# Expert numbers by thresholds and sums over ranks, expert groups block by block in turns, and an index table of two copies

## The chip, the cores and the metric

The kernel runs on one core of one Trainium2 chip. A core has five engines that run side by side, each with a queue of its own that is worked off in order: TensorE (PE, matmuls, with PEld for its weight loads), VectorE (DVE), ScalarE (ACT), GpSimd (POOL) and SyncE (SP, which only issues DMAs here). The metric is the device time of one execution in microseconds (us); lower is better. The kernel before takes 1928.7 us, the median of three runs (1924.66 to 1932.57).

## The reference

The program is two small transformer blocks over 256 tokens of width 1024 (float32): a mixer, a cross-attention and a PEER feed-forward layer in the first, two layers with a delta-rule mixer, an attention and a feed-forward net in the second. The change lies in the PEER layer. Each token has 8 retrieval heads; each head picks 16 out of 16384 experts by product keys.

```python
def peer_ffn(h, wq, subkeys, u, v):
    q = (xt @ wq).reshape(T, PEER_HEADS, 2, PEER_HALF)
    s = jnp.einsum('thpc,hpnc->thpn', q, subkeys).astype(jnp.float32)   # 2 x 128 scores a head
    s_top, i_top = lax.top_k(s, PEER_TOPK)                              # the 16 best of each half
    cand = s_top[:, :, 0, :, None] + s_top[:, :, 1, None, :]            # 16 x 16 sums
    cand_idx = i_top[:, :, 0, :, None] * PEER_N_KEYS + i_top[:, :, 1, None, :]
    best, pos = lax.top_k(cand.reshape(T, PEER_HEADS, PEER_TOPK * PEER_TOPK), PEER_TOPK)
    experts = jnp.take_along_axis(cand_idx.reshape(...), pos, axis=-1)
    gates = jax.nn.softmax(best, axis=-1).astype(h.dtype)
    # for every chosen expert e: y += gate * gelu(u[e] . x) * v[e]
```

## The kernel before

Activations lie with features on the 128 partitions and tokens along the row. Nearly all of the time goes to products with float32 weights at two-part precision: a class `Stream` brings all weights in one stream, 8 blocks of 128x128 to a tile, and splits each tile into a rounded part `whi` (ACT, L229) and the rest `wlo` (L231, a subtraction on DVE or POOL by the pattern `W.pat`; "DDP" means two tiles on DVE and the third on POOL). `mm3` (L253 to L256) makes three matmuls of each block: whi with the high part of the activations, whi with their low part, wlo with the high part. A tile feeds 24 matmuls. `whi` and `wlo` have three buffers each (`WB`), so ACT can write the `whi` of tile n+3 only when PE is done with tile n.

The PEER layer computes all 16384 experts for all tokens and masks them: `uphase` makes gelu(u.x) for 128 groups of 128 experts, two groups into the halves of one PSUM bank (`ps`), and `vphase` sums the products with v into four banks (`ys`). Phases run in the order u 0-64, u 64-96, v 0-32, u 96-128, v 32-64, v 64-128 (`PHASES`).

While PE does u 0-64, `topk` finds the experts on DVE, 128 tokens at a time (`tt` is 0 or 1). `both(uphase(0, 64), chain(topk...), TKR)` interleaves them when the program is written: after every tile of `uphase` (a `yield`), `TKR` (1.65) steps of `topk`, each ending in a `yield` of its own. `pace` lets a step's first instruction stand only behind the last DVE split of a tile. A framework then fixes the order on each engine. One call of `topk` does this:

- `top16` for 16 half-heads: the 16 best of 128 scores and their places (`top`, `idx`), by MAX8, FIND_INDEX8 and MATCH_REPLACE8.
- The 50 sums that can be among the 16 best of 256 (`PAIRS`: rank a of the first half goes with ranks 0 to 16/(a+1)-1 of the second) into `cv` on DVE, and their expert numbers into `ce` on POOL (L840).
- `top16` again for 8 heads over the 50 sums; `pos` is the place of each of the 16 winners in the 50, `psf` its float16 copy (L849).
- The expert number of each winner: for each head a table `eq` of 50 x 16 comparisons of `psf` with a counter `iom` (DVE, L856), its product with `ce` (`hit`, POOL, L860), and a sum over the 50 (`ex`, DVE, L864). Then the number is split into its first and second key, `f1` and `f2` (L871 to L875).
- The softmax of the gates.

Later `gates` builds the mask of the chosen experts from transposed `f1` and `f2`, on DVE and PE, beside u 64-96 and v 32-64.

Of the kernel before, what the change touches and what calls it, by code (L numbers as in the profile page):

```python
# [34 lines left out]
KC = 8  # L35
T1 = 256
# [8 lines left out]
LAG, MIXR, TKR, DLR = 2, 1.15, 1.65, 4  # L45
EXPAT = "DDP"
# [20 lines left out]
def _consts():  # L67
    i = np.arange(128)
    f = np.float32
    out, at = {}, {}  # L70
# [3 lines left out]
    c1, out = out, {}  # L74
# [24 lines left out]
    for s in (1, 2, 4, 8, 16, 32, 64):  # L99
        j, q = i[:, None], i[None, :]  # L100
# [3 lines left out]
    k = np.arange(T2)  # L104
# [36 lines left out]
def tile_two_blocks(ctx, tc, ws, xT, memT, metaT, par_d, wsm_d, subk_d, c1_d, cm_d, c2_d, out, dumps=None):  # L141
    nc = tc.nc
    dumps = dumps or {}
    V, G, A, PE = nc.vector, nc.gpsimd, nc.scalar, nc.tensor
# [99 lines left out]
    W = Stream()  # L244
# [497 lines left out]
    with tc.tile_pool(name="pe", bufs=1) as mp:  # L742
# [4 lines left out]
        nh, nl = operands(T1)  # L747
# [5 lines left out]
        iota = C1("iota")  # L753
# [48 lines left out]
        with tc.tile_pool(name="tk", bufs=1) as tp:  # L802
            def pace(r):

                after(r, W.last)
# [9 lines left out]
            NCAND = 50  # L815
            iom = tp.tile([128, NCAND, 8], F16, name="iom")
            V.tensor_copy(iom, iota[:, :NCAND].unsqueeze(2).to_broadcast([128, NCAND, 8]))

            fin = {}

            def topk(tt):
                top = tp.tile([128, 16, 16], F32, name="top")
                idx = tp.tile([128, 16, 16], U32, name="idx")
# [6 lines left out]
                iv = idf.rearrange("p (h z) k -> p h z k", z=2)  # L830
                V.tensor_scalar(iv[:, :, 0], iv[:, :, 0], 128.0, None, op0=OP.mult)
                cv = tp.tile([128, 8, NCAND], F32, name="cv")
                ce = tp.tile([128, 8, NCAND], F32, name="ce")
                o = 0
                for a, na, nb in PAIRS:
                    for e, dst, src in ((V, cv, tv), (G, ce, iv)):
                        d = dst[:, :, o:o + na * nb].rearrange("p h (a b) -> p h a b", a=na)
                        x = src[:, :, 0, a:a + na].unsqueeze(3).to_broadcast([128, 8, na, nb])
                        y = src[:, :, 1, :nb].unsqueeze(2).to_broadcast([128, 8, na, nb])
                        e.tensor_add(d, x, y)  # L840
                    o += na * nb
                    yield
# [7 lines left out]
                ex = tp.tile([128, 8, 16], F32, name="ex")  # L850
                W.pat = EXPAT
                hits = {}
                for h in range(9):
                    if h < 8:
                        eq = tp.tile([128, NCAND, 2, 8], F16, name="eq", bufs=2)
                        pace(V.tensor_tensor(eq, psf[:, h].rearrange("p (a b) -> p a b", a=2).unsqueeze(1).to_broadcast(  # L856
                            [128, NCAND, 2, 8]), iom.unsqueeze(2).to_broadcast([128, NCAND, 2, 8]),
                            op=OP.is_equal))
                        hits[h] = tp.tile([128, 16, NCAND], F32, name="hit", bufs=2)
                        G.tensor_mul(hits[h], eq.rearrange("p c a b -> p (a b) c"),  # L860
                                     ce[:, h].unsqueeze(1).to_broadcast([128, 16, NCAND]))
# [9 lines left out]
                V.tensor_copy(eu, ex.rearrange("p h k -> p (h k)"))  # L871
                V.tensor_scalar(i1, eu, 7, None, op0=OP.logical_shift_right)
                V.tensor_copy(f1, i1)
                V.tensor_scalar(i1, eu, 127, None, op0=OP.bitwise_and)
                V.tensor_copy(f2, i1)  # L875
# [713 lines left out]
def layout(a):  # L1589
# [7 lines left out]
    uT = a["peer_u"][0].reshape(128, 128, 8, 128).transpose(1, 2, 3, 0).reshape(128, 8, 128, 128)  # L1597
# [66 lines left out]
```

## Time and profile before

| what | value |
|---|---|
| median of three runs | 1928.7 us (1924.66 to 1932.57) |
| the profiled execution | 1923.93 us, its span 1922.2 us |
| PE busy | 1833.0 us, 95% of the span |
| DVE, ACT, POOL busy | 1327.3, 865.3, 645.8 us |
| granted TensorE clock, mean | 0.975 of full speed |
| the chain that ended last | PE 73%, DVE 20%, issue 4%, ACT and POOL 1% each |

Busy time of PE counts matmuls that overlap, so two stretches are better compared by how many matmuls they hold. A window's count takes in matmuls that cross its edges, some two per window. All times below are from this one execution; its stages are found by the tile names: u 0-64 runs from 351.6 to 553.5 us, u 96-128 from 766 to 857 us, the last v phase from 984 us on.

### The profile page before, as it was taken

To read this page: it belongs to the slowest core of one execution; us is meant where nothing else is said; L and a number is where in the kernel's file an instruction comes from. 1 tells how busy PE (TensorE), PEld (TensorE's weight loads), DVE (VectorE), ACT (ScalarE), POOL (GpSimd) and SP (SyncE) were. 2 spreads that over 40 slices of the span, in tenths; PEclk is the share of its full clock that TensorE was granted. 3 is DMA by queue.
4 is the path that set the end of the run, shared out by engine and by line. 5 is a ranking of instruction groups with operands and counts; after the bars stand their busy time and mean duration, and the time that the engine had idled before them with its cause. 6 is when DMAs were issued, how large, how long until landed. Compare 5 with 4: busy or idle time off the path is not lost.

```text
span 1922.2 us, 36981 instructions
## 1 busy us (share of the span) xinstructions
PE 1833.0 (95%) x15387; PEld 1766.3 (92%) x15387; DVE 1327.3 (69%) x2445; ACT 865.3 (45%) x1343; POOL 645.8 (34%) x394
## 2 busy tenths in 40 slices
PE   7999999989899999998899998899999999999999
PEld 6988999989898899998899998899899998679999
DVE  7746657789899965239965557854789845658872
ACT  5456554444343344443244444332444445644442
POOL 4312322364643322223322224321244431124442
PEclk9999999999999999999999998989999999989999
DMA  6432434444443355553355553211344543124453
GB/s 226 166 120 88 145 119 176 163 167 171 159 157 132 138 188 190 184 179 130 127 175 190 193 198 124 88 54 58 130 156 176 176 176 132 45 88 174 172 183 131
DMA packets 43128, 285.58 MB, mean 149 GB/s; under 512 B 5712, under 2 KB 8528, under 8 KB 9040
## 3 DMA queue, kind: packets, MB, share of 16 engines
q1 hardware_dynamic: 42960, 283.21, 41.8%
q8 instruction: 121, 1.98, 0.4%
q14 instruction: 47, 0.39, 0.1%
HBM read 282.14 MB, written 1.05 MB: 147 GB/s over the span
## 4 chain that ended last, share of the span: by engine, by line
PE 73%; DVE 20%; issue 4%; ACT 1%; POOL 1%; DMA 0%; SPq 0%; POOLq 0%; DVEq 0%; ACTq 0%
PE ps L254 16%; PE ps L256 16%; PE ps L255 16%; DVE wlo L231 5%; PE y L255 5%; PE y L256 5%; PE y L254 5%; DVE q L926 3%; DVE as L936 2%; DVE p L921 2%; DVE cy L979 1%; PE pa L1449 1%; DVE eq L923 1%; ACT whi L229 1%; DVE cy L437 1%
## 5 line engine op out<-in xcount | busy, mean ns | idle before, releaser
L229 ACT ACTIVATE whi<-raw 128x1024 fp32r<-128x1024 f32 x527 | 557.6, 1059 | 766.7 <-PE ps L255 506.5
L231 POOL TENSOR_TENSOR wlo<-raw,whi 128x1024 fp32r<-128x1024 f32 x190 | 473.9, 2494 | 914.6 <-ACT whi L229 914.4
L256 PE MATMUL ps<-xnh,wlo 128*128 128x256 f32 (+2 forms) x2336 | 678.0, 290 | 23.5 <-POOL wlo L231 15.8
L254 PE MATMUL ps<-xnh,whi 128*128 128x256 f32 (+2 forms) x2336 | 680.7, 292 | 13.8 <-ACT whi L225 6.8
L255 PE MATMUL ps<-xnl,whi 128*128 128x256 f32 (+2 forms) x2336 | 676.3, 290 | 0.8 <-DVE xnl L334 0.8
L231 DVE TENSOR_TENSOR wlo<-raw,whi 128x1024 fp32r<-128x1024 f32 x337 | 461.4, 1369 | 265.1 <-ACT whi L229 263.2
L256 PEld LDWEIGHTS ps<-xnh,wlo 128*128 128x128 f32 x2336 | 454.1, 194 | 29.6 <-POOL wlo L231 17.4
L254 PEld LDWEIGHTS ps<-xnh,whi 128*128 128x128 f32 x2336 | 454.1, 194 | 17.2 <-ACT whi L229 7.1
L255 PEld LDWEIGHTS ps<-xnl,whi 128*128 128x128 f32 x2336 | 453.1, 194 | 3.0 <-issue 1.6
L255 PE MATMUL y<-hl,whi 128*128 128x256 f32 x1024 | 285.5, 279 | 7.7 <-DVE hl L406 7.7
L254 PE MATMUL y<-hh,whi 128*128 128x256 f32 x1024 | 287.5, 281 | 0.0
L256 PE MATMUL y<-hh,wlo 128*128 128x256 f32 x1024 | 284.7, 278 | 1.7 <-DVE wlo L231 1.7
L255 PEld LDWEIGHTS y<-hl,whi 128*128 128x128 f32 x1024 | 194.4, 190 | 9.1 <-DVE hl L406 9.1
L256 PEld LDWEIGHTS y<-hh,wlo 128*128 128x128 f32 x1024 | 194.2, 190 | 1.9 <-DVE wlo L231 1.9
L254 PEld LDWEIGHTS y<-hh,whi 128*128 128x128 f32 x1024 | 194.1, 190 | 0.0
L254 PE MATMUL ps<-fh,whi 128*128 128x272 f32 (+1 forms) x352 | 100.1, 284 | 0.0
L256 PE MATMUL ps<-fh,wlo 128*128 128x272 f32 (+1 forms) x352 | 100.1, 284 | 0.0
L255 PE MATMUL ps<-fl,whi 128*128 128x272 f32 (+1 forms) x352 | 100.0, 284 | 0.0
L406 DVE TENSOR_TENSOR hl<-as,hh 128x512 fp32r<-128x512 f32 x64 | 72.3, 1131 | 32.9 <-ACT hh L405 32.9
L979 DVE SCALAR_TENSOR_TENSOR cy<-xpad,par,cy 128x272 f32<-128x272 f32 (+1 forms) x132 | 90.2, 691 | 2.6
L254 PEld LDWEIGHTS ps<-fh,whi 128*128 128x128 f32 x352 | 66.3, 188 | 0.0
L255 PEld LDWEIGHTS ps<-fl,whi 128*128 128x128 f32 x352 | 66.3, 188 | 0.0
(527 smaller groups left out, 2728.3 us busy)
## 6 DMA issues: line engine op xcount, KB each, us to landing
raw<-in_ws_dram SPq DMA_DIRECT2D x263, 1024.0 KB, 4.8
X<-in_xT_dram SPq DMA_DIRECT2D x4, 256.0 KB, 4.5
memX<-in_memT_dram SPq DMA_DIRECT2D x1, 1024.0 KB, 13.1
as<-in_subk_d_dram SPq DMA_DIRECT2D x1, 1024.0 KB, 6.9
out_dram<-X SPq DMA_DIRECT2D x4, 256.0 KB, 2.4
c<-in_c_d_dram SPq DMA_DIRECT2D x1, 793.0 KB, 4.3
cm<-in_cm_d_dram SPq DMA_DIRECT2D x1, 776.0 KB, 10.9
raw<-in_ws_dram SPq DMA_DIRECT2D x4, 128.0 KB, 4.4
```

The source lines that it names most:

```text
L229: A.activation(hi, s, AF.Copy)
L231: r = e.tensor_sub(lo, s, hi.bitcast(F32))
L254: PE.matmul(ps, wh, xh, start=start, stop=False, **k)
L255: PE.matmul(ps, wh, xl, start=False, stop=False, **k)
L256: PE.matmul(ps, wl, xh, start=False, stop=stop, **k)
L406: V.tensor_sub(lo, x, hi.bitcast(F32))
L437: V.scalar_tensor_tensor(y, xpad[:, j:j + T1], P("conv_w", 4 * m + j), y, op0=OP.mult, op1=OP.add)
L921: V.tensor_tensor(p1, index(0, 128), pairs(i1T, 128), op=OP.is_equal)
L923: V.tensor_tensor(eq, index(R * r, R), pairs(i2T, R), op=OP.is_equal)
L926: V.tensor_mul(q[:, z], eq, pairs(gT[:, z], R))
L936: V.tensor_mul(a, a, pv[:, 32 * s:32 * s + 32])
L979: V.scalar_tensor_tensor(dst, xpad[:, j:j + T], P(wname, o + j), dst, op0=OP.mult, op1=OP.add)
```

## The change

Three edits. First, `topk` finds the two keys of each winner without the expert numbers of the candidates. The 50 places are grouped by the rank of the first half, and the groups start at thresholds 0, 16, 24, 29, 33 ... (`thr`). For each winner, `ge` holds 16 comparisons "place >= threshold"; the sum of `ge` times the steps between thresholds is the start of its group, place minus start is its rank in the second half (`rb_`), the sum of `ge` times the differences of successive first indices (`d1`) is the first key, and the sum of "rank equals `rb_`" times the second indices (`d2`) is the second. A sum over 16 is made by halving (`fold`). All of it is float16 on DVE, for all 8 heads at once (2048 elements a row). The tables `d1` and `d2` hold every index twice side by side. POOL does none of it.

Second, `uphase` takes the two groups of a bank in turns, block by block (k outside, z inside), with one start flag for the bank; the weights are laid out to match. Third, `TKR` is 1.5, and the constant tile `c1` grows by 32 columns for `thr` and `dthr`.

```diff
-LAG, MIXR, TKR, DLR = 2, 1.15, 1.65, 4
-EXPAT = "DDP"
+LAG, MIXR, TKR, DLR = 2, 1.15, 1.5, 4
...
+    thr = np.concatenate([[0], np.cumsum([16 // (a + 1) for a in range(15)])]).astype(f)
+    out["thr"] = np.broadcast_to(thr[None], (128, 16)).copy()
+    out["dthr"] = np.broadcast_to(np.diff(thr, prepend=f(0))[None], (128, 16)).copy()
...
-                for z in range(2):
-                    for k in range(KC):
+                for k in range(KC):
+                    for z in range(2):
                         wh, wl = W.block()
-                        mm3(ps[:, z * T1:(z + 1) * T1], wh, wl, nh[:, k], nl[:, k], k == 0, k == KC - 1)
-                    yield
+                        mm3(ps[:, z * T1:(z + 1) * T1], wh, wl, nh[:, k], nl[:, k], k == 0 and z == 0, k == KC - 1,
+                            skip_group_check=True)
+                    if k % 4 == 3:
+                        yield
...
-            iom = tp.tile([128, NCAND, 8], F16, name="iom")
-            V.tensor_copy(iom, iota[:, :NCAND].unsqueeze(2).to_broadcast([128, NCAND, 8]))
-
+
+            thr, dthr, rank = (tp.tile([128, 16, 16], F16, name=n) for n in ("thr", "dthr", "rank"))
...
-                idf = tp.tile([128, 16, 16], F32, name="idf")
-                V.tensor_copy(idf, idx)
+
+                iv = idx.rearrange("p (h z) k -> p h z k", z=2)
+                ix = tp.tile([128, 2, 8, 16], F16, name="ix")
+                V.tensor_copy(ix, iv.rearrange("p h z k -> p z h k"))
+                d1 = tp.tile([128, 8, 16, 2], F16, name="d1")
+                d2 = tp.tile([128, 8, 16, 2], F16, name="d2")
+                V.tensor_copy(d1[:, :, 0], ix[:, 0, :, :1].to_broadcast([128, 8, 2]))
+                for e in range(2):
+                    V.tensor_sub(d1[:, :, 1:, e], ix[:, 0, :, 1:], ix[:, 0, :, :15])
+                V.tensor_copy(d2, ix[:, 1].unsqueeze(3).to_broadcast([128, 8, 16, 2]))
+                yield
...
-                for h in range(9):
-                    if h < 8:
-                        eq = tp.tile([128, NCAND, 2, 8], F16, name="eq", bufs=2)
-                        pace(V.tensor_tensor(eq, psf[:, h].rearrange("p (a b) -> p a b", a=2).unsqueeze(1).to_broadcast(
-                            [128, NCAND, 2, 8]), iom.unsqueeze(2).to_broadcast([128, NCAND, 2, 8]),
-                            op=OP.is_equal))
-                        hits[h] = tp.tile([128, 16, NCAND], F32, name="hit", bufs=2)
-                        G.tensor_mul(hits[h], eq.rearrange("p c a b -> p (a b) c"),
-                                     ce[:, h].unsqueeze(1).to_broadcast([128, 16, NCAND]))
-                        yield
-                    if h:
-                        pace(V.reduce_sum(ex[:, h - 1], hits.pop(h - 1), axis=AX.X))
-                        yield
...
+                def fold(x, out):
+
+                    n = 8
+                    while n > 1:
+                        V.tensor_add(x[:, :, :n], x[:, :, :n], x[:, :, n:2 * n])
+                        n //= 2
+                        if n == 4:
+                            yield
+                    V.tensor_add(out, x[:, :, 0], x[:, :, 1])
+                    yield
+
+                ge, x = cells("ge"), cells("gx")
+                pace(V.tensor_tensor(ge, slots16(psf), over_h(thr), op=OP.is_ge))
+                yield
+                pace(V.tensor_mul(x, ge, over_h(dthr)))
+                yield
+                rb_ = tp.tile([128, 8, 16], F16, name="rb_")
+                yield from fold(x, rb_)
+                V.tensor_sub(rb_, psf, rb_)
+                weighted(x, ge, d1)
+                yield
+                yield from fold(x, f1.rearrange("p (h k) -> p h k", h=8))
+                pace(V.tensor_tensor(ge, slots16(rb_), over_h(rank), op=OP.is_equal))
+                yield
+                weighted(x, ge, d2)
+                yield
+                yield from fold(x, f2.rearrange("p (h k) -> p h k", h=8))
```

Two places in the order of the instructions. The first is VectorE from the eighth head's last step to the gates, for the first 128 tokens. Before:

```order
L849 CAST psf<-pos 128x128
L856 TENSOR_TENSOR eq<-psf,iom 128x800
L231 TENSOR_TENSOR wlo<-raw,whi 128x1024
L856 TENSOR_TENSOR eq<-psf,iom 128x800
L864 TENSOR_REDUCE ex<-hit 128x16
L231 TENSOR_TENSOR wlo<-raw,whi 128x1024
L856 TENSOR_TENSOR eq<-psf,iom 128x800
L864 TENSOR_REDUCE ex<-hit 128x16
L856 TENSOR_TENSOR eq<-psf,iom 128x800
L231 TENSOR_TENSOR wlo<-raw,whi 128x1024
L864 TENSOR_REDUCE ex<-hit 128x16
```

VectorE in the changed kernel (`gx` is the tile that `fold` halves, `d_4381` is `d1`; the split of a weight tile is now on L234):

```order
L858 CAST psf<-pos 128x128
L889 TENSOR_TENSOR ge<-psf,thr 128x2048
L891 TENSOR_TENSOR gx<-ge,dthr 128x2048
L881 TENSOR_TENSOR gx<-gx 128x8x128
L881 TENSOR_TENSOR gx<-gx 128x8x64
L234 TENSOR_TENSOR wlo<-raw,whi 128x1024
L881 TENSOR_TENSOR gx<-gx 128x8x32
L885 TENSOR_TENSOR rb__4813<-gx 128x128
L895 TENSOR_TENSOR rb__4813<-psf,rb__4813 128x128
L234 TENSOR_TENSOR wlo<-raw,whi 128x1024
L873 TENSOR_TENSOR gx<-ge,d_4381 128x2048
```

From the first comparison to the last sum six splits of weight tiles stood before, a seventh behind them; now four stand there, a fifth behind, and at most five `topk` instructions lie between two splits. Nothing on VectorE waits for GpSimd's `hit` any more.

The second place is GpSimd over the whole of u 0-64. Before, for the first 128 tokens:

```order
L840 TENSOR_TENSOR ce<-idf 128x8x8
L231 TENSOR_TENSOR wlo<-raw,whi 128x1024 x3
L860 TENSOR_TENSOR hit<-eq,ce 128x800 x3
L231 TENSOR_TENSOR wlo<-raw,whi 128x1024
L860 TENSOR_TENSOR hit<-eq,ce 128x800 x3
L231 TENSOR_TENSOR wlo<-raw,whi 128x1024
L860 TENSOR_TENSOR hit<-eq,ce 128x800 x2
L231 TENSOR_TENSOR wlo<-raw,whi 128x1024 x5
```

In the changed kernel GpSimd has this between the squares of the PEER norm and those of the next block's norm:

```order
L359 TENSOR_TENSOR sq<-X 128x256 x2
L234 TENSOR_TENSOR wlo<-raw,whi 128x1024
L359 TENSOR_TENSOR sq<-X 128x256
L234 TENSOR_TENSOR wlo<-raw,whi 128x1024 x101
L1062 TENSOR_TENSOR gin<-X 128x256 x2
```

All 30 instructions of `ce` and `hit` are gone from its queue; only its splits of weight tiles are left.

## Rows read from the trace of the kernel before

**Rows 1.** The page's busy time by engine: us, share of the span, instructions.
```profile
PE 1833.0 (95%) x15387; PEld 1766.3 (92%) x15387; DVE 1327.3 (69%) x2445; ACT 865.3 (45%) x1343; POOL 645.8 (34%) x394
```
**Rows 2.** Windows: us, busy (x) by engine, PE clock, DMA share, GB/s.
```profile
351.60:414.10 62.50, 62.50 (x530) 62.50 (x530) 55.62 (x221) 28.23 (x33) 28.32 (x16) 1.00 0.52 183
414.10:442.00 27.90, 20.38 (x146) 19.77 (x145) 26.23 (x19) 7.81 (x9) 23.27 (x9) 0.88 0.32 113
442.00:510.20 68.20, 68.20 (x578) 68.20 (x577) 59.50 (x232) 34.16 (x39) 29.02 (x18) 1.00 0.52 182
510.20:527.30 17.10, 11.75 (x75) 11.37 (x74) 16.15 (x11) 4.15 (x5) 14.24 (x6) 0.80 0.40 138
527.30:553.50 26.20, 26.20 (x225) 26.20 (x224) 21.18 (x39) 14.36 (x16) 14.32 (x6) 1.00 0.45 162
553.50:673.00 119.50, 110.19 (x1260) 107.02 (x1259) 118.69 (x206) 40.62 (x47) 41.67 (x16) 0.99 0.40 137
```
**Rows 3.** Who waited for whom (total, times, longest us), 404-442 and 500-530.
```profile
PE ps L256 <- POOL wlo L231: 7.3, 2, 4.7
...
PE ps L256 <- POOL wlo L231: 5.3, 1, 5.3
```
**Rows 4.** GpSimd in time order: start, us, line, what [idle before].
```profile
404.03 2.44 POOL L231 TENSOR_TENSOR wlo<-raw,whi 128x1024 fp32r<-128x1024 f32 x1 [6.11 <-ACT whi L229]
...
428.23 2.33 POOL L860 TENSOR_TENSOR hit<-eq,ce 128x800 f32<-128x800 f16 x1 [0.58 <-DVE eq L856]
430.49 3.35 POOL L231 TENSOR_TENSOR wlo<-raw,whi 128x1024 fp32r<-128x1024 f32 x1
```
**Rows 5.** VectorE in time order, the same stretch.
```profile
404.13 2.43 DVE L849 CAST psf<-pos 128x128 f16<-128x128 uint32 x1
...
408.22 2.83 DVE L856 TENSOR_TENSOR eq<-psf,iom 128x800 f16<-128x800 f16 x1
...
418.09 3.36 DVE L231 TENSOR_TENSOR wlo<-raw,whi 128x1024 fp32r<-128x1024 f32 x1
421.37 0.97 DVE L864 TENSOR_REDUCE ex<-hit 128x16 f32<-128x800 f32 x1
```
**Rows 6.** Durations by line: ns min/median/max, first and last start.
```profile
L856 DVE TENSOR_TENSOR eq<-psf,iom x16: 562/1930/2828, 406.6 to 530.5; 128x800 f16<-128x800 f16 x16
L864 DVE TENSOR_REDUCE ex<-hit x16: 971/973/987, 411.0 to 535.9; 128x16 f32<-128x800 f32 x16
L849 DVE CAST psf<-pos x2: 219/1323/2427, 404.1 to 499.7; 128x128 f16<-128x128 uint32 x2
```
**Rows 7.** POOL groups of 351.6-553.5: busy us, mean ns | idle before.
```profile
L860 POOL TENSOR_TENSOR hit<-eq,ce 128x800 f32<-128x800 f16 x16 | 45.2, 2825 | 10.5 <-DVE eq L856 9.9 <-PE ps L255 0.6
```
**Rows 8.** Durations of the weight splits in u 0-64, and ACT's from the page.
```profile
L231 DVE TENSOR_TENSOR wlo<-raw,whi x42: 1204/1222/3483, 358.0 to 549.1; 128x1024 fp32r<-128x1024 f32 x42
L231 POOL TENSOR_TENSOR wlo<-raw,whi x22: 2382/2427/4877, 351.7 to 551.9; 128x1024 fp32r<-128x1024 f32 x22
...
L229 ACT ACTIVATE whi<-raw 128x1024 fp32r<-128x1024 f32 x527 | 557.6, 1059 | 766.7 <-PE ps L255 506.5
```
**Rows 9.** Durations of nearby VectorE forms, as rows 6.
```profile
L923 DVE TENSOR_TENSOR eq<-io,i2T x64: 407/413/2512, 548.2 to 966.9; 128x512 f16<-128x512 f16 x64
L921 DVE TENSOR_TENSOR p<-io,i1T x64: 675/678/2927, 547.6 to 971.8; 128x1024 f16<-128x1024 f16 x64
L880 DVE TENSOR_TENSOR gt<-best x2: 271/272/274, 403.9 to 499.5; 128x128 f32<-128x128 f32 x2
L840 DVE TENSOR_TENSOR cv<-top x14: 176/200/2233, 381.5 to 478.4; 128x64 f32<-128x64 f32 x4, 128x128 f32<-128x128 f32 x2, 128x40 f32<-128x40 f32 x2, 128x32 f32<-128x32 f32 x2
```
**Rows 10.** Windows as rows 2: u 96-128, the last v phase, the cross-attention's output.
```profile
780.00:840.00 60.00, 60.00 (x510) 60.00 (x509) 17.17 (x14) 27.42 (x32) 17.12 (x8) 1.00 0.51 182
1000.00:1140.00 140.00, 140.00 (x1238) 140.00 (x1237) 73.36 (x60) 68.49 (x78) 40.81 (x17) 1.00 0.56 195
...
284.00:291.00 7.00, 7.00 (x61) 7.00 (x60) 5.53 (x11) 3.93 (x7) 1.15 (x2) 1.00 0.57 171
```

More of the change, by code (lines that the diff above doesn't have):

```diff
@@ L752, in tile_two_blocks @@
         V.tensor_copy(io2, C1("iota").unsqueeze(2).to_broadcast([128, 128, 2]))
-        iota = C1("iota")
         a0 = asub().rearrange("p a b -> p (a b)")
@@ L815, in tile_two_blocks @@
             NCAND = 50
-            iom = tp.tile([128, NCAND, 8], F16, name="iom")
-            V.tensor_copy(iom, iota[:, :NCAND].unsqueeze(2).to_broadcast([128, NCAND, 8]))
+            thr, dthr, rank = (tp.tile([128, 16, 16], F16, name=n) for n in ("thr", "dthr", "rank"))
+            for t, c in ((thr, C1("thr")), (dthr, C1("dthr")), (rank, C1("iota")[:, :16])):
+                V.tensor_copy(t, c.unsqueeze(2).to_broadcast([128, 16, 16]))
             fin = {}
@@ L826, in topk @@
                     yield
-                idf = tp.tile([128, 16, 16], F32, name="idf")
-                V.tensor_copy(idf, idx)
+                iv = idx.rearrange("p (h z) k -> p h z k", z=2)
[8 more added lines that the diff above has]
+                yield
                 tv = top.rearrange("p (h z) k -> p h z k", z=2)
-                iv = idf.rearrange("p (h z) k -> p h z k", z=2)
-                V.tensor_scalar(iv[:, :, 0], iv[:, :, 0], 128.0, None, op0=OP.mult)
                 cv = tp.tile([128, 8, NCAND], F32, name="cv")
-                ce = tp.tile([128, 8, NCAND], F32, name="ce")
                 o = 0
                 for a, na, nb in PAIRS:
[L836 to L840, printed above, removed]
+                    V.tensor_add(cv[:, :, o:o + na * nb].rearrange("p h (a b) -> p h a b", a=na),
+                                 tv[:, :, 0, a:a + na].unsqueeze(3).to_broadcast([128, 8, na, nb]),
+                                 tv[:, :, 1, :nb].unsqueeze(2).to_broadcast([128, 8, na, nb]))
                     o += na * nb
@@ L849, in topk @@
                 V.tensor_copy(psf, pos)
-                ex = tp.tile([128, 8, 16], F32, name="ex")
-                W.pat = EXPAT
-                hits = {}
-                for h in range(9):
-                    if h < 8:
-                        eq = tp.tile([128, NCAND, 2, 8], F16, name="eq", bufs=2)
-                        pace(V.tensor_tensor(eq, psf[:, h].rearrange("p (a b) -> p a b", a=2).unsqueeze(1).to_broadcast(
-                            [128, NCAND, 2, 8]), iom.unsqueeze(2).to_broadcast([128, NCAND, 2, 8]),
-                            op=OP.is_equal))
-                        hits[h] = tp.tile([128, 16, NCAND], F32, name="hit", bufs=2)
-                        G.tensor_mul(hits[h], eq.rearrange("p c a b -> p (a b) c"),
-                                     ce[:, h].unsqueeze(1).to_broadcast([128, 16, NCAND]))
-                        yield
-                    if h:
-                        pace(V.reduce_sum(ex[:, h - 1], hits.pop(h - 1), axis=AX.X))
-                        yield
@@ L866, in topk @@
-                W.pat = "DDP"
-                eu = tp.tile([128, 128], U32, name="eu")
-                i1 = tp.tile([128, 128], U32, name="i1")
                 f1 = tp.tile([128, 128], F32, name="f1", bufs=2)
                 f2 = tp.tile([128, 128], F32, name="f2", bufs=2)
[L871 to L874, printed above, removed]
@@ L875, in topk, with cells, over_h, slots16 @@
-                V.tensor_copy(f2, i1)
+                def cells(name):
+                    return tp.tile([128, 8, 16, 16], F16, name=name)
+                def over_h(c):
+                    return c.unsqueeze(1).to_broadcast([128, 8, 16, 16])
+                def slots16(x):
+                    return x.unsqueeze(2).to_broadcast([128, 8, 16, 16])
+                def weighted(x, mask, d):
+                    pace(V.tensor_mul(x.rearrange("p h j (s e) -> p (h j) s e", e=2),
+                                      mask.rearrange("p h j (s e) -> p (h j) s e", e=2),
+                                      d.rearrange("p h j e -> p (h j) e").unsqueeze(2).to_broadcast([128, 128, 8, 2])))
@@ L1596, in layout @@
            _blocks(a["peer_wq"][0])]
-    uT = a["peer_u"][0].reshape(128, 128, 8, 128).transpose(1, 2, 3, 0).reshape(128, 8, 128, 128)
+    uT = a["peer_u"][0].reshape(128, 64, 2, 8, 128).transpose(1, 3, 2, 4, 0).reshape(128, 8, 128, 128)
     vv = a["peer_v"][0].reshape(128, 128, 8, 128).transpose(1, 2, 0, 3).reshape(128, 8, 128, 128)
```

## The prediction

> **What bounds the kernel now.** I read the busy times first: PE is busy for 95% of the span, DVE for 69%, POOL for 34% [rows 1]. PE sets the end almost everywhere, so an edit on DVE or POOL is worth what PE waits for it, and no more. Next came the windows over u 0-64, where `topk` runs beside PE [rows 2]. Count matmuls there. In the first 62.5 us PE ran 530, less about two that cross the edges: 528, or 22 tiles, at 118.4 ns each, with the clock at full rate. The same pace holds from 442.0 to 510.2 (576 matmuls) and from 527.3 to 553.5 (222). Between lie two holes. The one of 27.9 us holds 144 matmuls, which take 144 x 118.3 ns = 17.0 us at the steady pace: 10.9 us lost. The one of 17.1 us holds 72, worth 8.5 us: 8.6 us lost. Together 19.5 us, and that includes the slower clock in them: the granted share is 0.88 and 0.80 there and 1.00 around, so some of the matmuls ran at 1.2 GHz in place of 2.4 after PE had stood still.
>
> The holes are where `eq`, `hit` and `ex` run. The waits name the cause: PE stood for POOL's `wlo`, 7.3 us in two pieces in the first hole and 5.3 us in one in the second [rows 3]. POOL's queue shows why [rows 4]: its split of 430.49 stood behind a `hit` of 2.33 us and then took 3.35 us where the median is 2.43 [rows 8]. DVE was late there too: a cast that takes 219 ns at its quickest took 2427 [rows 6], from 404.13 to 406.56, while POOL had a split from 404.03 to 406.47; an `eq` of 562 ns at its quickest took 2.83 us and a split 3.36 us in place of 1.22 [rows 5, 6, 8]. The reductions never grew (971 to 987 ns). So in this trace a DVE instruction with two inputs in SBUF, or this cast, and a POOL instruction exclude each other for a whole instruction.
>
> **What a late split costs.** With three buffers, ACT starts on the `whi` of tile n+3 when PE is done with tile n; two tiles, 5.68 us, are then left. ACT takes 1.06 us, DVE's split 1.22, POOL's 2.43 [rows 8]. The cover is 5.68 - 1.06 - 1.22 = 3.4 us for a DVE split and 2.2 us for one on POOL. A `hit` of 2.8 us ahead of POOL's split is more than 2.2; that is the hole.
>
> **Part 1, removed and added.** Gone for each half of the tokens: 8 `hit` on POOL (16 are 45.2 us [rows 7], so 22.6 a half) and seven `ce` additions; on DVE 8 `eq` at a median of 1.93 us (about 14 us) and 8 reductions at 0.97 (7.8 us), with five small casts and shifts.
> Added on DVE: five instructions over 2048 float16 elements. Their form (runs of at least two neighbours, the rest repeated) is that of `eq` and `p`: 407 ns for 512 elements, 678 for 1024 [rows 9], so 0.53 ns an element and 678 + 1024 x 0.53 = 1220 ns for 2048. Three foldings of 1024, 512, 256 and 128 elements: 0.68 + 0.41 + 0.27 + 0.27 = 1.63 us each, the last one at the 272 ns of a float32 addition of 128. With a subtraction: 5 x 1.22 + 3 x 1.63 + 0.27 = 11.3 us. The tables `ix`, `d1` and `d2` are five instructions of 120 to 256 elements, of 0.2 to 0.3 us by the same rows: 1.3 us. They stand beside the additions to `cv`, of which the longest took 2233 ns with a median of 200 [rows 9] while POOL had `ce`; those waits go, so I cost the tables at nothing (1.3 us a half if DVE had no slack).
>
> **What is late next.** POOL's queue holds only splits, so POOL's hole goes. DVE's eleven steps now lie among splits alone. From `psf` to the end of the gates (four small instructions, 0.9 us at the 0.2 to 0.3 of rows 9) DVE has 0.2 + 11.3 + 0.9 = 12.4 us of `topk` and six splits, 7.3 us; PE runs nine tiles meanwhile, 25.6 us, and POOL makes three splits, 7.3 us. Even if POOL and DVE never overlapped, the sum is 27.0 against 25.6: 1.4 us too much, once per half, against a cover of 3.4. At most five `topk` instructions (2.9 us) lie between two splits, with one POOL split 5.3 us, against 5.68 when the interval holds a POOL tile. I expect no hole, and leave 0.5 us a half for a split that comes late: 19.5 - 1.0 = 18.5 us gained. Ends: 19.5 if nothing waits; what the lock rival below leaves at the other.
> The Trainium skill ("SBUF — State Buffer", section Who interferes with whom) speaks against this edit: a DVE instruction with two SBUF inputs contends with a GpSimd instruction that reads SBUF, a reduction never does. The change swaps 7.8 us of reductions a half for additions that do. The rows agree on both kinds; by the rule alone the 1.4 us a half would count, and the gain would be 16.7 us.
>
> **TKR.** The chain had 100 steps (49 a half and two to finish), 64 tiles x 1.65 = 106; now 92, and 64 x 1.5 = 96. It ends at tile 61 either way: nothing.
>
> **Part 2, block by block in turns.** Matmuls, bytes and splits are the same; only the pace of PE can change. Three paces stand in the trace [rows 10], counts less two or three at the edges: u 96-128 has 508 in 60 us, 118.2 ns; the v phase 1236 in 140 us, 113.3 ns; the cross-attention's output product 58.5 in 7 us, 119.6 ns. All have 256 columns and a full clock. In v the moving operand stays for 24 matmuls while the output moves every three; in u and in the attention's product it is the reverse. The new u changes the output every three and the moving operand every six. Bounds for 1536 + 768 = 2304 matmuls (u 64-96 is left out: there DVE is busy 118.7 of 119.5 us [rows 2] and PE waits for it): (118.2 - 113.3) x 2304 = 11.3 us gained, (119.6 - 118.2) x 2304 = 3.2 us lost. Nearest is u itself, with the same tiles at the same distances; I take 2 us gained, since half of the changes of the moving operand go.
> The Trainium skill ("TensorE: Matmul & The Clock Gate", section Back-to-back issue gap) gives 262 cycles for 256 columns, 109 ns at 2.4 GHz as an estimate, whatever the order; all three rows lie above it and differ, so the trace doesn't bear it out. By it this part is worth 0 and the sum 2 us less.
>
> **Part 3, the larger constants.** 32 columns more lengthen one DMA of 793 KB by 16 KB off the path: nothing. They move every later tile by 128 bytes; see the last rival.
>
> **Sum.** 18.5 + 2 = 20.5 us off the profiled execution's 1923.9 (span 1922.2 and 1.7 around it): 1903.4. The median is 1928.7, 4.8 above that execution; from it the sum gives 1908.2. I name 1906, between the two.
>
> **Rivals.**
> Lock bound (chance 0.12): POOL's splits become late because every DVE instruction around them has two inputs. If each of the three POOL splits of a half waits a whole DVE instruction, 1.22, and holds back the next, the excess is 1.4 + 3 x 1.22 = 5.1 us; past the cover PE stops for 1.7 to 5, and the clock may fall again for some 3 (the first hole lost 10.9 us on 7.3 of waits). Price 5 to 8 us a half; gain 20.5 - 13 = 7: 1917 from the profiled execution. For it: rows 5 and 6 show such waits. Against: POOL's share of the stretch falls from 23.3 of 27.9 us to about a quarter.
> Pace of v (0.12): u 0-64 and 96-128 go to 113.3 ns; 11.3 in place of 2, 1894. For it: v's outputs take turns as u's will. Against: in v the moving operand rests four times as long.
> It doesn't do what it says (0.05): the 2048-element forms go at one element at a time, as float32 does: 1.22 us for 1024 [rows 8], 2.3 for 2048. 8 us more DVE a half, past the cover by 6; the holes stay, 1919 to 1924. Against: the innermost pairs are those of rows 9.
> Slower (0.04): the 128 bytes put PE's operands where products run at 119.6. v's 3072 matmuls lose 6.3 ns each, 19.4 us, u's 2304 lose 3.2, and some 7400 others of PE's 15387 instructions [rows 1] 1.4 each, 10 us: 33 - 18.5 = 14 slower, 1938. It decides from a v pace of 113.3 + 18.5/3072 us = 119.3 ns. For it: paces do differ between tiles of one shape. Against: all tiles move together, so distances stay.
> The rest (0.67) is the forecast, 1900 to 1913.
>
> **How the numbers follow.** 0.5% is 9.6 us, about what a measurement can tell from no change. Faster by more: the forecast, the v pace and half of the lock rival, 0.67 + 0.12 + 0.06 = 0.85. Within 0.5%: the other half of the lock and the rival of forms, 0.06 + 0.04 = 0.10. Slower: 0.05. The range must hold 8 in 10: it takes the forecast (0.67), most of the lock rival down to a gain of 8 and the upper part of the v pace: 1894 to 1917.
>
> **What would show it.** Right: 144 matmuls of the old first hole in about 17 us, granted clock 1.00 through u 0-64, no PE wait for POOL's split over 1 us, `ge` at about 1.22 us when it stands free. u 96-128 with 508 to 520 matmuls in 60 us; over 525 the v pace, under 504 a loss. v still at 1236 in 140 us; 1180 would be the last rival. The forecast is wrong if a hole of over 3 us stays in either half, or if `ge` takes over 2 us without a POOL split beside it.

## The result, and the profile after

The changed kernel takes 1905.63 us, the median of four runs (1899.51 to 1914.36), against 1926.78 for the kernel before beside it (four runs, 1924.66 to 1932.57): a ratio of 0.9889, 95% interval 0.9843 to 0.9935. The prediction said 1906, with 1894 to 1917 as its range. The profiled execution took 1907.24 us, its span 1905.5, so 16.7 us less span than before. The interval of the ratio allows a gain of 12.5 to 30.3 us, so stages are told apart by the profiles and not by the medians.

The page's busy times of the changed kernel answer to [rows 1]:
```profile
PE 1827.8 (96%) x15387; PEld 1762.8 (93%) x15387; DVE 1301.9 (68%) x2447; ACT 865.7 (45%) x1343; POOL 597.1 (31%) x364
```
POOL has lost its 30 instructions and 49 us, DVE 25 us, PE only 5 us of busy time. What fell is PE's standing still. The windows over u 0-64 show it; the columns are those of [rows 2], and the first two rows answer to its first two, the third to its fourth and fifth:
```profile
348.20:410.00 61.80, 61.80 (x530) 61.80 (x530) 50.19 (x225) 28.22 (x33) 19.52 (x8) 1.00 0.53 186
410.00:426.80 16.80, 16.80 (x146) 16.80 (x145) 16.52 (x17) 7.83 (x9) 5.76 (x3) 1.00 0.49 168
494.20:528.60 34.40, 34.40 (x297) 34.40 (x296) 31.12 (x43) 18.54 (x21) 11.06 (x5) 1.00 0.52 185
348.20:528.60 180.40, 180.40 (x1545) 180.40 (x1545) 152.90 (x515) 88.76 (x102) 56.04 (x22) 1.00 0.53 187
```
The stretch of the first hole now holds the same 146 matmuls in 16.8 us where it took 27.9, PE is busy throughout, and the granted clock is 1.00 in place of 0.88. The last row is the whole of u 0-64: 180.4 us with no gap in PE, where 351.6 to 553.5 was 201.9. The waits of this stretch (total, times, longest us; the first three) have no line for PE where [rows 3] had POOL's split; it is POOL and DVE that now wait for ACT's `whi`, and ACT for PE:
```profile
POOL wlo L234 <- ACT whi L232: 131.6, 22, 7.3
ACT whi L232 <- PE ps L258: 87.9, 58, 2.1
DVE wlo L234 <- ACT whi L232: 21.7, 10, 4.3
```
VectorE in time order where [rows 5] stood (start, us, line, what):
```profile
408.34 1.22 DVE L889 TENSOR_TENSOR ge<-psf,thr 128x2048 f16<-128x2048 f16 x1
409.60 3.31 DVE L891 TENSOR_TENSOR gx<-ge,dthr 128x2048 f16<-128x2048 f16 x1
412.95 1.15 DVE L881 TENSOR_TENSOR gx<-gx 128x1024 f16<-128x1024 f16 x2
414.01 1.22 DVE L234 TENSOR_TENSOR wlo<-raw,whi 128x1024 fp32r<-128x1024 f32 x1
...
417.00 3.43 DVE L873 TENSOR_TENSOR gx<-ge,d 128x2048 f16<-128x2048 f16 x1
```
and GpSimd beside it, as [rows 4]:
```profile
408.48 3.34 POOL L234 TENSOR_TENSOR wlo<-raw,whi 128x1024 fp32r<-128x1024 f32 x1 [6.03 <-ACT whi L232]
416.89 2.46 POOL L234 TENSOR_TENSOR wlo<-raw,whi 128x1024 fp32r<-128x1024 f32 x1 [5.07 <-ACT whi L232]
```
`ge`, which stands free, takes 1.22 us. The product at 409.60 has the same size and takes 3.31: POOL's split ran to 411.82, and 411.82 + 1.2 is the product's end within about 0.1 us. POOL's split in turn took 3.34 where 2.43 is usual, since it met `ge`. That is the mutual exclusion of [rows 4 to 6], seen again. The durations by line over u 0-64 (ns min/median/max), as [rows 6, 8, 9]:
```profile
L889 DVE TENSOR_TENSOR ge<-psf,thr x2: 1224/1224/1224, 408.3 to 492.5; 128x2048 f16<-128x2048 f16 x2
...
L873 DVE TENSOR_TENSOR gx<-ge,d x4: 3428/3430/3432, 417.0 to 509.8; 128x2048 f16<-128x2048 f16 x4
...
L881 DVE TENSOR_TENSOR gx<-gx x18: 284/425/693, 412.9 to 514.4; 128x1024 f16<-128x1024 f16 x6, 128x512 f16<-128x512 f16 x6, 128x256 f16<-128x256 f16 x6
...
L234 DVE TENSOR_TENSOR wlo<-raw,whi x42: 1204/1218/1227, 354.9 to 523.8; 128x1024 fp32r<-128x1024 f32 x42
```
All six weighting products (one of L891 and two of L873 a half) lost 2.1 to 2.2 us to a split on POOL; none of the 42 splits on DVE did, where before the longest took 3483 ns.

**Where 16.7 us come from.** Stage by stage, cut at the first matmul of each (us of the two profiled spans):

| stage | before | after | difference |
|---|---|---|---|
| up to u 0-64 | 351.6 | 348.2 | -3.4 |
| u 0-64 | 201.9 | 180.4 | -21.5 |
| u 64-96 | 122.2 | 124.0 | +1.8 |
| v 0-32 | 90.1 | 93.3 | +3.2 |
| u 96-128 | 90.9 | 89.9 | -1.0 |
| the rest | 1065.5 | 1069.7 | +4.2 |

So u 0-64 and u 96-128 gave 22.5 us, and the others took back 5.8 on balance. Of these the change alters only u 64-96 by more than the shift: there, too, the groups go in turns, but PE waits for DVE. The windows of u 64-96 and v 0-32, before:
```profile
553.50:675.70 122.20, 112.89 (x1283) 109.72 (x1281) 121.36 (x212) 41.70 (x50) 41.67 (x16) 0.99 0.40 139
...
688.00:765.50 77.50, 77.50 (x686) 77.50 (x686) 40.41 (x33) 37.13 (x43) 24.00 (x10) 1.00 0.55 192
```
and after:
```profile
528.60:652.60 124.00, 114.55 (x1283) 111.95 (x1281) 122.63 (x217) 41.73 (x50) 42.40 (x16) 0.96 0.38 137
...
665.00:746.00 81.00, 81.00 (x690) 81.00 (x689) 40.63 (x33) 37.16 (x43) 24.04 (x10) 1.00 0.53 184
```
In u 64-96 the granted clock was 0.96 in place of 0.99. In v 0-32 the clock was full and PE never stood, yet the pace was 81.0 us / 688 = 117.7 ns against 77.5 / 684 = 113.3. The experiments below show that neither is a fixed price of the change: the granted clock of u 64-96 lay between 0.95 and 0.99 over all profiles, with the old `topk` as with the new one, and the changed kernel ran v 0-32 at 113.3 ns in its second profile.

### The profile page after: what moved, and what is told of

Read it like the earlier page. It is cut to its first block, busy times and chain, and to the rows that moved or that the text cites. A ratio compares the mean times of both kernels' runs of the same rounds, so it can differ in the third digit from the quotient of the medians.

```text
span 1905.5 us, 36942 instructions
## 1 busy us (share of the span) xinstructions
PE 1827.8 (96%) x15387; PEld 1762.8 (93%) x15387; DVE 1301.9 (68%) x2447; ACT 865.7 (45%) x1343; POOL 597.1 (31%) x364
## 4 chain that ended last, share of the span: by engine, by line
PE 75%; DVE 19%; issue 4%; ACT 2%; POOL 1%; DMA 0%; SPq 0%; POOLq 0%; DVEq 0%; ACTq 0%
PE ps L257 17%; PE ps L258 16%; PE ps L259 16%; PE y L259 5%; PE y L257 5%; PE y L258 5%; DVE wlo L234 4%; DVE q L954 3%; DVE p L949 2%; DVE as L964 2%; DVE cy L1007 1%; DVE eq L951 1%; PE pa L1477 1%; DVE acc L363 1%; DVE cy L440 1%
## 5 line engine op out<-in xcount | busy, mean ns | idle before, releaser
L234 POOL TENSOR_TENSOR wlo<-raw,whi 128x1024 fp32r<-128x1024 f32 x190 | 477.8, 2515 | 955.9 <-ACT whi L232 955.6
L234 DVE TENSOR_TENSOR wlo<-raw,whi 128x1024 fp32r<-128x1024 f32 x337 | 439.4, 1304 | 271.8 <-ACT whi L232 270.1
L259 PEld LDWEIGHTS ps<-xnh,wlo 128*128 128x128 f32 x2336 | 450.4, 193 | 16.8 <-DVE wlo L234 9.5
L954 DVE TENSOR_TENSOR q<-eq,gT 128x512 f16<-128x512 f16 x128 | 66.3, 552 | 0.0
```

Source lines behind the costliest of these rows:

```text
L234: r = e.tensor_sub(lo, s, hi.bitcast(F32))
L954: V.tensor_mul(q[:, z], eq, pairs(gT[:, z], R))
```

## The experiments

Paces come from stage lengths in the profiles. Where PE has no hole, u 0-64 and u 96-128 repeat to 0.1 us; with holes u 0-64 doesn't (201.9 and 200.3 us with the same PEER code, see the third kernel), and v 0-32 doesn't either. The medians carry several us of scatter, much of it from stages with a lower granted clock. u 0-64 has 1536 matmuls of weights, u 96-128 has 768.

**The edits apart.** The first kernel is the changed one with the old order of u and the old layout of the weights; it keeps the new search for the keys, `TKR` at 1.5 and the larger constants:
```diff
-                for k in range(KC):
-                    for z in range(2):
+                for z in range(2):
+                    for k in range(KC):
...
```


> The changed kernel with the old order of the expert groups (z outside, k inside, old weight layout); thresholds, ranks, tables and TKR as in the change. Theory (GpSimd's queue made the holes, and only the first edit removes them): u 0-64 takes 64 tiles x 2.84 us = 182 us, with no hole, against 201.9 before and 180.4 changed; u 96-128 stays at 90.9 us as before. Time some 2 to 3 us above the changed kernel, 1908. Rival (the order of the groups took part in closing the holes, by changing when splits are wanted): holes come back in part, u 0-64 above 186 us.

1906.12 us (1904.01 to 1907.13, four runs), ratio 0.9875, 0.9825 to 0.9925. Its windows of u 0-64 and u 96-128:
```profile
348.50:531.00 182.50, 182.50 (x1545) 182.50 (x1544) 153.27 (x515) 88.78 (x103) 58.78 (x22) 1.00 0.52 184
...
743.40:834.30 90.90, 90.90 (x770) 90.90 (x770) 26.35 (x22) 41.74 (x48) 25.20 (x11) 1.00 0.54 186
```
u 0-64 lost 19.4 us against the 201.9 before and no hole is left, u 96-128 is as before. The median ratio is that of the whole change (0.9889) within the noise.

The second is the kernel before with the new order of u alone (the same lines the other way round, and the weights laid out to match).

> The kernel before with only the expert groups block by block in turns. Theory (this edit is worth the pace of PE alone): tiles of 2.81 us in place of 2.84 where PE isn't stopped, the two holes of u 0-64 stay (19 to 20 us), u 0-64 at about 200 us, u 96-128 at 89.8 against 90.9; time 2 to 3 us under the kernel before, 1924. Rival: the holes shrink by more than 3 us and the time is 1920 or less.

1926.41 us (ten runs), ratio 0.9993, 0.9956 to 1.003: nothing that the median can tell. Its windows, of u 0-64, the first hole and u 96-128:
```profile
351.70:552.90 201.20, 186.81 (x1545) 185.41 (x1544) 182.02 (x518) 88.81 (x103) 109.13 (x52) 0.97 0.47 167
...
414.00:442.00 28.00, 21.72 (x154) 21.12 (x154) 26.81 (x17) 7.81 (x9) 22.83 (x9) 0.88 0.32 114
...
764.80:854.60 89.80, 89.80 (x770) 89.80 (x770) 26.33 (x22) 41.75 (x48) 25.24 (x11) 1.00 0.55 188
```
The holes stay (and so do PE's waits for POOL's split, 12.1 us in four pieces), while u 96-128 is 1.1 us shorter. The order is worth that much, and 182.5 - 180.4 = 2.1 us in u 0-64 where `TKR` is 1.5. Here, with `TKR` at 1.65, a small new hole stands in u 0-64 beside the old ones: the tile at 379.9 took 4.7 us. PE's wait there, and the two splits behind it on POOL and DVE:
```profile
PE ps L256 <- DVE wlo L231: 1.6, 1, 1.6
```
```profile
378.37 2.38 POOL L231 TENSOR_TENSOR wlo<-raw,whi 128x1024 fp32r<-128x1024 f32 x1 [5.23 <-ACT whi L229]
...
378.44 3.39 DVE L231 TENSOR_TENSOR wlo<-raw,whi 128x1024 fp32r<-128x1024 f32 x1
```
In the kernel before, DVE's split of this tile came first:
```profile
378.26 1.21 DVE L231 TENSOR_TENSOR wlo<-raw,whi 128x1024 fp32r<-128x1024 f32 x1
...
378.48 3.25 POOL L231 TENSOR_TENSOR wlo<-raw,whi 128x1024 fp32r<-128x1024 f32 x1 [5.53 <-ACT whi L229]
```

The third is the kernel before with 32 more columns of constants:
```diff
+    out["pad32"] = np.zeros((128, 32), f)
```


> The kernel before with 32 columns of zeros more in the constant tile, so that every later tile lies 128 bytes further on. Theory (PE's pace depends on how operands lie to each other, or not on addresses at all): the paces stay, u 96-128 at 118.2 ns a matmul (90.9 us), the last v phase at 113.3 (1236 in 140 us). Rival (the absolute address counts): one of them moves by 2 ns or more, 1.5 us in u 96-128 or 3 us in the last 140 us of v.

1925.33 us in one run. u 96-128 took 90.9 us and v 0-32 took 90.1, both as before, and the last v phase stayed at 113.3 ns. The shift by 128 bytes changes no pace. Its window of u 0-64:
```profile
349.90:550.20 200.30, 188.95 (x1545) 187.77 (x1544) 179.44 (x519) 88.74 (x103) 109.46 (x52) 0.97 0.47 168
```
With its two holes the stage took 200.3 us, 1.6 less than the 201.9 of the kernel before, whose PEER code is the same. Against the 182.5 us without them the holes cost 17.8 us here and 19.4 there, and a tenth of a microsecond means nothing in them.

**POOL's queue or DVE's own work?** The kernel before, without `ce` and `hit` on POOL; DVE keeps its eight comparisons and eight sums a half:
```diff
-                    for e, dst, src in ((V, cv, tv), (G, ce, iv)):
+                    for e, dst, src in ((V, cv, tv),):
...
-                        hits[h] = tp.tile([128, 16, NCAND], F32, name="hit", bufs=2)
-                        G.tensor_mul(hits[h], eq.rearrange("p c a b -> p (a b) c"),
-                                     ce[:, h].unsqueeze(1).to_broadcast([128, 16, NCAND]))
+                        hits[h] = eq.rearrange("p c a b -> p (a b) c")
```


> The kernel before without GpSimd's part of the expert search: the additions to ce and the products hit are left out, and the sums over 50 are taken of the comparisons themselves, so expert numbers and what follows from them are not the reference's. VectorE keeps all its 8 comparisons and 8 sums a half. Theory (GpSimd's queue and its exclusion of VectorE made the holes): both holes go, u 0-64 at 182 to 184 us, comparisons at 0.56 us unless a GpSimd split is running. Rival (VectorE's own work was too much): 8 x (0.56 + 0.97) is 12.3 us a half, as much as the changed kernel's 11.3, but if the number of steps and splits on VectorE made the holes they stay at 5 us or more each, u 0-64 above 190 us.

1916.51 us in one run. Its window of u 0-64, and the comparisons in it:
```profile
347.00:529.50 182.50, 182.50 (x1545) 182.50 (x1544) 162.32 (x519) 88.75 (x103) 54.11 (x22) 1.00 0.52 184
```
```profile
L856 DVE TENSOR_TENSOR eq<-psf,iom x16: 555/574/2779, 402.0 to 507.4; 128x800 f16<-128x800 f16 x16
```
The stage is as long as with the keys alone, and the median `eq` falls from 1930 to 574 ns. The holes were POOL's part of the search, its `hit` above all, ahead of its splits and against DVE; the run takes both effects away together and doesn't tell them apart. DVE's own comparisons and sums cost PE nothing, though each sum now took 1.74 us in place of 0.97. `TKR` is 1.65 here and the order old, so neither 1.5 nor the turns are needed to close the holes. That the whole run is 10 us longer than the keys alone goes with its mean granted clock, 0.972 against 0.978 (0.006 x 1910 = 11 us), in other stages.

**TKR.** The changed kernel with `TKR` at 1.65:

> The changed kernel with TKR 1.65 as before in place of 1.5: the chain of topk's steps then ends at tile 56 of 64 in place of 61. The prediction costs TKR at nothing: u 0-64 at 180.4 us within 0.5. Rival: with the steps closer together more topk instructions lie between two splits, so that a DVE split comes late behind a GpSimd split; holes of 1 to 3 us come back and the stage takes 182 to 186 us.

1913.09 us in one run. u 0-64 took 182.6 us, 2.2 more. Most of it is the tile at 376.5, which took 4.6 us in place of 2.81. (The tile at 504.6 took 3.4, but there PE ran the six transposes of the found keys and gates, L924, which the changed kernel runs in two later tiles; that makes about 0.2 of the difference.) PE's only wait for a split in the stage, then the two splits behind it, on POOL and DVE, in time order:
```profile
PE ps L259 <- DVE wlo L234: 1.5, 1, 1.5
```
```profile
374.85 2.39 POOL L234 TENSOR_TENSOR wlo<-raw,whi 128x1024 fp32r<-128x1024 f32 x1 [4.91 <-ACT whi L232]
...
375.23 3.09 DVE L234 TENSOR_TENSOR wlo<-raw,whi 128x1024 fp32r<-128x1024 f32 x1
```
In the changed kernel the splits there were these:
```profile
373.62 1.21 DVE L234 TENSOR_TENSOR wlo<-raw,whi 128x1024 fp32r<-128x1024 f32 x1
...
374.80 2.41 POOL L234 TENSOR_TENSOR wlo<-raw,whi 128x1024 fp32r<-128x1024 f32 x1 [5.58 <-ACT whi L232]
```
With 1.65 the split on DVE stands behind more `topk` instructions, starts 1.6 us later, falls into POOL's split and waits it out. So the prediction's zero for `TKR` was wrong by 2.2 us in the changed kernel: it looked at where the chain ends, not at which split meets which. It is 1.65 together with the turns that costs this: the same tile's split is late in the kernel with the turns alone, and in none of the three profiles with 1.65 and the old order, the third of which (without `ce` and `hit`) took the same 182.5 us as the keys with 1.5. At 1.65 the turns would have gained nothing in u 0-64: 182.6 us against 182.5.

**What sets PE's pace in u?** `nh` and `nl` have rows of 1088 bytes for each k, so the eight rows start at 0, 64, 128 and 192 bytes modulo 256 in turn. Four places were tried with dense rows of 1024 bytes, which start alike (N is 0, 48, 16 or 32; the turns are kept):
```diff
-        nh, nl = operands(T1)
+        nh, nl = (xp.tile([128, KC, T2], F32R, name=n, bufs=1).rearrange("p k t -> p (k t)")[:, N:N + KC * T1]
+                  .rearrange("p (k t) -> p k t", k=KC) for n in ("xnh", "xnl"))
```


> The changed kernel with one thing different: the two parts of the PEER activations (nh, nl) are stored densely, 256 columns (1024 bytes) a row of k in place of 272 (1088 bytes), so that each of the eight rows of k starts at the same place modulo 256 bytes, the place at which the attention's output product stands (119.6 to 120 ns a matmul). In the changed kernel u 0-64 takes 180.4 us (1536 matmuls, 117.5 ns) and u 96-128 takes 89.8 (116.9 ns); the rows of k there stand at 0, 64, 128 and 192 bytes in turn. Theory A (the pace of PE depends on where the moving operand starts modulo 256 bytes, whatever the order of the blocks): all rows go at 120 ns, u 0-64 takes 184 us, u 96-128 takes 92. Theory B (the pace of u comes from the turns and from how often the moving operand changes): 180.4 and 89.8, within 0.8 us.

> As the kernel before it, dense rows of 1024 bytes, but all of them moved by 192 bytes (48 columns), to the place modulo 256 bytes at which v's activations stand in the stretches at 113.3 ns. Theory A (place of the moving operand): u 0-64 falls from 180.4 to 174 us (1536 x 113.3 ns) and u 96-128 from 89.8 to 87.0; 9.2 us less than the changed kernel, about 1897 us. Theory B (turns and changes of the operand): 180.4 and 89.8 stay, about 1906 us. A third: v goes in two paces with the same tiles (117.7 ns beside 113.3 ns in the profile of the changed kernel), so the pace may be either of the two in each stage, whatever the place.

> The changed kernel with the old order of u (a group whole, then the other) and the rows of k dense at 192 bytes. With the old order and the old places u 0-64 took 182.5 us and u 96-128 took 90.9. Theory A: the place alone sets the pace, 174 and 87 us. Theory B: the order sets it, 182.5 and 90.9. If order and place both count, it lies between, and with the kernel before it in this list it splits the two effects.

> Dense rows moved by 64 bytes. The theory of the place (120 ns at 0 bytes, 113.3 or 117.7 at 192) expects one constant pace over all 24 matmuls of a tile, other than 120: the rows of the changed kernel at this place went at 117.8, so u 0-64 181 us and u 96-128 90.5, or 87 if this place too has a quick pace. The rival (only the place at 0 is bad, anything else is as 192): u 96-128 at 87.0.

> Dense rows moved by 128 bytes. As for 64 bytes: the rows of the changed kernel at this place went at 117, so u 96-128 at about 90 us by the theory of the place, 87.0 if every place but 0 has the quick pace.

| kernel | u 0-64, us | u 96-128, us | u 96-128, ns a matmul | time, us |
|---|---|---|---|---|
| changed (0, 64, 128, 192 in turn) | 180.4 | 89.8 | 117.0 | 1905.63, four runs |
| dense at 0 bytes | 185.0 | 92.1 | 120.0 | 1917.29, one run |
| dense at 64 | 181.7 | 90.5 | 117.8 | 1904.86, one run |
| dense at 128 | 183.0 | 91.1 | 118.7 | 1907.56, one run |
| dense at 192 | 181.6 | 87.0 | 113.3 | 1903.07, four runs |
| dense at 192, old order | 181.6 | 87.0 | 113.3 | 1898.68, one run |

The times of the changed kernel and of the dense ones weren't all taken side by side; against the kernel before beside it (1922.06 us) dense at 192 has a ratio of 0.9900, 0.985 to 0.995, no better than the changed kernel's. The windows of the two stages, dense at 0:
```profile
348.50:533.50 185.00, 185.00 (x1545) 185.00 (x1544) 153.57 (x518) 88.66 (x103) 57.61 (x22) 1.00 0.50 182
744.80:836.90 92.10, 92.10 (x771) 92.10 (x770) 26.33 (x22) 41.67 (x48) 25.30 (x11) 1.00 0.50 183
```
dense at 192:
```profile
350.60:532.20 181.60, 181.60 (x1546) 181.60 (x1545) 153.33 (x518) 88.69 (x103) 55.25 (x22) 1.00 0.50 185
746.70:833.80 87.10, 87.10 (x771) 87.10 (x770) 26.33 (x22) 41.76 (x48) 25.20 (x11) 1.00 0.54 194
```
and with the old order of u:
```profile
350.10:531.70 181.60, 181.60 (x1546) 181.60 (x1545) 153.31 (x515) 88.70 (x103) 55.23 (x22) 1.00 0.51 185
745.80:832.90 87.10, 87.10 (x771) 87.10 (x770) 26.33 (x22) 41.77 (x48) 25.22 (x11) 1.00 0.53 194
```
PE busy throughout, clock full, the same matmuls, and 5 us between the first two in u 96-128: where `nh` and `nl` start within their tiles sets that stage's pace. Where all rows start alike, tried at 192, the order of the blocks is worth nothing (last two). But u 0-64 with the very tiles of u 96-128 stays at 117.8 ns a matmul, so place is not all, and the 174 us expected of it didn't come; VectorE is far busier there (153 us of 181.6 against 26 of 87). The 117.8 ns of the place at 64 is the same as this slower pace at 192, so one profile can't tell whether that place is slower or the stage fell into the slower pace. Nor is it the plain address: the third kernel moved every later tile by half of 256 bytes, and v's pace stayed. The distance to some other operand, which no dense variant holds fixed, is a rival that wasn't tested.

The starts of the single matmuls in u 96-128 show where the turns gain. With the turns six matmuls in a row read one row of k; at the place 192 they stand 122, 116, 114, 113, 113 and 113 ns apart (medians, the same in all four profiles with the turns and the old rows). In the old order three read it, 118 or 119, 120 and 119 ns apart. The gain lies in the rows at 192 and 128, and next to none in those at 0 and 64.

**Once more, unchanged**: the kernel with dense rows at 192 bytes, and the changed kernel, measured side by side.

> The kernel with dense rows moved by 192 bytes once more, unchanged. In its first profile u 0-64 went at 117.7 ns (181.6 us) and u 96-128 at 113.3 ns (87.0 us), with the same tiles. Theory C (at this place a stretch falls into one of two paces, by chance at its start): u 0-64 is at either, 174 or 181.6 us, and at least one of the stretches u 0-64, v 0-32, u 96-128 differs from the first profile. Theory D (what runs beside it sets which of the two): u 0-64 at 181.6 and u 96-128 at 87.0 again. Against the changed kernel: 1 to 3 us less by u 96-128 alone, not to be told apart in the medians; about 9 less if u 0-64 falls to 174.

> The changed kernel once more, unchanged, to see which stages repeat. Expected in both theories: u 0-64 at 180.4 us without a hole, u 96-128 at 89.8. Theory C: v 0-32, at 117.7 ns a matmul in the first profile, is at 113.3 or 117.7 by chance. Theory D: v 0-32 at 117.7 again. Time 1900 to 1910 us, ratio to the kernel before 0.985 to 0.993.

Dense at 192: 1902.05 us (1899.62 to 1911.42, six runs), ratio to before 0.9871, 0.9826 to 0.9916; u 0-64 181.6 and u 96-128 87.0 us again. The changed kernel: 1906.74 us (1900.30 to 1913.39, six runs), ratio 0.9887, 0.9842 to 0.9932. Its windows of u 0-64 and v 0-32:
```profile
346.80:527.20 180.40, 180.40 (x1545) 180.40 (x1544) 152.84 (x515) 88.81 (x103) 56.02 (x22) 1.00 0.52 186
...
652.10:742.20 90.10, 87.58 (x770) 87.19 (x769) 50.21 (x44) 43.20 (x50) 26.70 (x11) 1.00 0.52 187
```
u 0-64 repeats to 0.1 us; v 0-32 took 93.3 us in the first profile and 90.1 here, in the same program, so the 117.7 that theory D expected there didn't come. v's slower pace is no fixed price of the change. Two more profiles have it: rows at 64 bytes (v 0-32 93.4 us), and `TKR` at 1.65, where the stage took only 91.5 because PE stood less at its start, but ran at 117.8 ns:
```profile
660.00:740.00 80.00, 80.00 (x681) 80.00 (x681) 39.15 (x34) 36.99 (x43) 23.31 (x10) 1.00 0.54 193
```
In the other eleven profiles the pace was 113.3. The slower one came in three of the ten profiles with the new `topk` and in none of the four with the old; whether the change makes it likelier is open. For u 0-64 at 192 bytes three profiles of three gave the slower pace and for u 96-128 three the quicker; whether something beside it sets that, or what it started with, stays open, and theory D, which was expected to explain both, holds for u and not for v. By its stages the dense kernel is worth 2.8 - 1.2 = 1.6 us more than the changed one; the two ranges overlap, and the medians don't tell them apart.

## Why the prediction was right, step by step

- **The holes.** Predicted 19.5 us in them, 18.5 gained. The keys (with `TKR` at 1.5) took 19.4 off u 0-64. The half microsecond a half left for a late split wasn't needed. That 19.4 meets 19.5 to 0.1 is luck: by the profile of the third kernel the same holes are worth 17.8.
- **POOL's queue as the cause.** Confirmed by taking `ce` and `hit` away and nothing from DVE: the same 182.5 us. How much was `hit` standing ahead of POOL's splits, and how much `hit` shutting DVE out, no run shows; PE's waits in u 0-64 were 12.7 us for POOL's split and 0.2 for DVE's.
- **The new work on DVE.** Predicted 1.22 us for 2048 elements and 1.63 for a folding; measured 1.22, and 0.69 + 0.43 + 0.28 + 0.29 = 1.69 (the last is one of 291 or 292 ns; for `rb_` it is 224, so that folding takes 1.62).
- **The exclusion, three times a half.** The prediction added POOL's 7.3 us to DVE's path as if the two never overlapped, against a cover of 3.4. Measured 3 x 2.2 = 6.6 us. It landed on the weighting products and not on splits, and PE had no wait. The section Who interferes with whom of "SBUF — State Buffer" in the Trainium skill says that a VectorE instruction with two inputs in SBUF contends with a GpSimd instruction that reads there; the 3.31 and 3.43 us agree. Counting that as a loss, 16.7 in place of 18.5, was too dark, for none of it reached PE.
- **Turns.** Predicted 2 us gained between -3.2 and 11.3; measured 2.1 + 1.0 = 3.1, the 2.1 only with `TKR` at 1.5. The 2 was a choice within its bounds, so the nearness is luck. The reason given, fewer changes of the moving operand, holds at most in part: with rows that start alike the order is worth 0. With rows at four places the gaps between matmuls at 192 come down to 113 or 114 ns only after two matmuls at one row, which fits fewer changes between places; why a change of place costs anything wasn't isolated.
- **TKR.** Predicted 0, measured 2.2 us in the changed kernel (one profile), hidden in the sum because the better value was the one used. With the old order of u no cost shows; it comes from 1.65 and the turns together.
- **Constants and shift.** Predicted 0, measured 0 (the third kernel).
- **The rivals.** The lock bound fell with PE's missing wait, the pace of v with 516 matmuls in 60 us of u 96-128 where it needed over 525, the rival of forms with `ge` at 1.22 us, the slower one with v's last phase, still 1238 in 140 us. These are the rows for the last and for u 96-128, as [rows 10]:
```profile
760.00:820.00 60.00, 60.00 (x516) 60.00 (x515) 17.16 (x14) 28.10 (x33) 17.68 (x8) 1.00 0.50 182
980.00:1120.00 140.00, 140.00 (x1238) 140.00 (x1237) 73.37 (x60) 68.67 (x78) 40.78 (x17) 1.00 0.55 195
```
- **The total.** 20.5 us were summed. The two stages gave 22.5, the other stages took back 5.8 net in this pair of profiles, by clock and v's pace. The medians differ by 21.15, within 12.5 to 30.3, and by 18.3 in the second measurement of the changed kernel. So the sum is borne out, but that the 1906 named meets 1905.63 is luck: it was put halfway between two bases 4.8 us apart, and single runs went from 1899.51 to 1914.36.

## What to carry to other kernels

Count the holes by matmuls: a window's length less its matmuls at the neighbour's pace is what an edit off the critical engine can give back; here 19.5 us were counted, and 17.8 or 19.4 came back, by which profile with holes one takes. A long GpSimd instruction can cost twice, once in its own queue ahead of work that PE needs and once by shutting VectorE out; look which work is behind it and whether a wait of 2 us falls on an instruction with cover. Where an interleaving rate or the order of blocks is changed, ask which instruction will stand beside which, not only where the chain ends: a split on VectorE that began 0.2 us before GpSimd's took 1.21 us, one that began 0.07 us behind took 3.39.

## What the runs showed of the hardware

With 256 columns, full clock and the same engines busy, PE's steady pace in u 96-128 went from 113.3 (offset 192 bytes) over 117.8 (64) and 118.7 (128) to 120.0 ns a matmul (0) by where the moving operand starts within its tile. That the offset counts by itself, and not the distance to another operand, isn't shown; moving every later tile by 128 bytes changed nothing. In v 0-32 the same program went at 117.7 ns in one profile and 113.3 in another, with the same tiles, and held that pace once PE ran without a stop. The Trainium skill's figure for an isolated matmul of this width ("TensorE: Matmul & The Clock Gate", Back-to-back issue gap, 262 cycles, an estimate of 109 ns at 2.4 GHz) lies below all of these; these are steady streams, so they don't test it in the way the prediction took them to.
The length of u 64-96 varied from 120.5 to 126.5 us over the fourteen profiles and didn't follow the edits; differences of that size in a single profile of this kernel say nothing.
